# Substitution paced by the projections, a block of the joins by VectorE's transposes, and attention's position biases scaled block by block

## The chip, the cores and the metric

The kernel runs on one core of one Trainium2 chip. The core's engines each work through a queue of their own: TensorE (PE, with its weight loads shown as PEld), VectorE (DVE), ScalarE (ACT), GpSimd (POOL) and SyncE (SP), which here mostly issues DMA transfers. An instruction waits for semaphores that other engines or transfers raise; whatever is queued behind it on its engine waits too. The metric is the time of one execution on the device, in microseconds (us).

## The reference

Two layers run over 1024 tokens of width 1024 in fp32. Layer 0 mixes by a gated MLP (half the width) and by a gated DeltaNet (the other half), layer 1 by differential attention; each layer then has an MLP (square of relu, width 4096) and a gated addition of per-layer embeddings (PLE). What the change touches:

```python
# gated DeltaNet, per head and chunk of c = 64 tokens (4 heads, 16 chunks)
a = where(strict, einsum(k_beta, k) * decay, 0)   # strictly lower triangular
t_mat = a + eye(c)
u = solve_triangular(t_mat, v_beta)               # unit diagonal, lower
w = solve_triangular(t_mat, k_beta * exp(gc))
...                                               # then a scan over the chunks with a state
# differential attention, per head h of 8 (two softmaxes r = 0, 1), blocks of 128 queries
logits = q @ k.T - slopes[h] * dist               # slopes[h] = 2 ** -(h + 1)
logits = where(dist >= 0, logits, -inf)
attn = softmax(logits[0]) - lam * softmax(logits[1])
o = attn @ v
# MLP
h = h + square(relu(rms_norm(h) @ w_mlp1)) @ w_mlp2
```

## The kernel before

**Matmuls.** Nearly all time goes to products in three passes (`mm3`, L76 is the line of every matmul, L79 that of every transpose on TensorE): weights and activations are split into a high and a low part, and high x high, high x low and low x high are added up in PSUM. A weight's parts are made by `split` (L222 to L224): ScalarE casts the high part (L223), VectorE subtracts it to get the low part (L224). A tile of a weight (`w`, or `g` for the MLP's combined weights) is therefore ready only when an instruction on ScalarE and one on VectorE have run, in their places in those queues.

**Order.** A scheduler gives each engine its order from priorities and estimated times; the class `Ordered` (L48 to L90) adds constraints of issue order. `behind(inst, mark)` says that `inst` may be issued only after the instruction `mark` was issued on its own engine; it carries no semaphore for data. `pe.mark` is the name of the matmul written last. `floor` puts all matmuls of a group behind the group before.

**Layer 0's mixing** (`even_mix`, from L1231) has two kinds of work. The projections of the layer are a stream of *fill units* (small groups of `mm3`, `proj_qkv`, `proj_z`, `proj_uv`), which `pump(n)` (L1825) issues in order up to number n. The DeltaNet's own work is written between them, and with `run` (L1852) at high priority (EARLY = 3000). The counts of units issued in the stages are FILLA, FILLB, FILLC and FILLD (L35).
- `ahead(c)` (L1568 to L1607) makes the triangular system of each 128-token block c (two chunks); TensorE's `pd`, `pk`, `pkk`; the strictly lower blocks `am` lie in the tile `ring`. Its diagonal blocks of 32x32 are stored to `diag` (L1605) and the whole to `am_dram` (L1606), through SyncE's queue.
- `solve()` (L1612 to L1642) loads all 128 diagonal blocks, one per partition, into `work` (L1617, two transfers, for `x` and `a`), and issues loads of off-diagonal blocks, `ay` (L1621) and `a64` (L1628). It then inverts the blocks by forward substitution, all on VectorE: 30 columns, each a multiply `outer` (L1634) and an addition into `work` (L1635). Each depends on the one before. Two transposes of 128x1024 (L1640, L1641) give `dt` and `d`, the inverses block by block and their transposes.
- `merge()` (L1644 to L1712) joins 32x32 inverses to 64x64 and these to 128x128. At the first level, `py` = (off-diagonal block) x (inverse); then `pz` for p = 0 and 1, the two halves of the blocks: the product `pz[z0]` = d-transposed x `ay` is the joined block. For p = 0 a second product, `pz[z1]` = `ay`-transposed x d, gives the same block transposed. VectorE copies `pz[z0]` into `xt` (L1689, tile name `xts`), ScalarE copies `pz[z1]` into `xn` (L1691). The second level does the same with blocks of 64 (`py` and `yt` L1700, `pz` and the copies L1709), and stores the result to `xt_dram`. All products here are plain fp32 of 32x32 or 64x64; each shows as two matmul records. The names `quad[u][0]` (z0) and `quad[u][1]` (z1) are 32-partition strips of the half u.
- `prep(c)` and `step(c)` then run the scan over the blocks, with the rest of the projections as fill. VectorE also does the convolution behind some projections (`cx` L1353, `t` L1359, `qkv` L1362).

**The MLP** (`mlp`, from L290) multiplies by seven products of half-size blocks; `product2(2)` (L542) is its last one, and its sums go into `acc` (L284 and the additions behind it).

**Attention** (`attention`, from L873) keeps the position biases in one tile `al` (128x1024): GpSimd writes distances by `iota` (L880) and sets what lies in the future to -1e30 by `affine_select` (L881). As the slope halves from head to head, VectorE multiplies the whole of `al` by 0.5 at each head's first block (L1005, `b == 0 and r == 0`). For each block b of 128 queries and each r, `logits` runs the products `qk` and one VectorE operation that adds `al` and takes the minimum (`lg` and `nm`, L1016); block b reads the columns of `al` from (7-b)*128 on. ScalarE takes the exponential (L1019), VectorE combines the two (L1025 to L1027), TensorE transposes and multiplies by the values (`po`). `olo` (L1074) is the low part of a head's transposed result.

## Time and profile before

| | |
|---|---|
| three runs | 2529.52, 2530.80 and 2535.22 us, median 2530.80 |
| the profiled execution | 2532.05 us |
| its span in the trace | 2530.3 us, at a granted TensorE clock of 0.999 |
| 0 to 143 us | first projections and `ahead` |
| 143 to 188 us | substitution beside projections: TensorE busy 42.23 of 45 us, granted clock 0.96 |
| 188 to 250 us | joins and the first scan steps: TensorE busy 60.38 of 62 us, clock 0.97 |
| 250 to 440 us | rest of layer 0's mixing: 188.31 of 190 us, clock 1.00 |
| 440 to 1112 us | layer 0's MLP, from 936 us on its last part: 669.73 of 672 us |
| 1300 to 1700 us | seven of attention's heads: 395.97 of 400 us |

A profile row such as "L1005 DVE TENSOR_SCALAR al<-al x8" names the line, the engine, the operation, the tile written and the tiles read, and how many there were. In a list by time the first two numbers are the start and the duration, in us from the span's start, and "[2.77 <-DVE w L224]" says that the engine had been idle for 2.77 us and which instruction's end released it. In the chain of waits each row is a start, a length and what the chain spent it on; "SPq" is SyncE's queue, "issue" is time for which the profile shows no cause. Durations of neighbouring instructions overlap, since an engine starts the next one before the last has written back: what an instruction costs its engine is the distance from its start to the next start.

### The profile page before, as it was taken

How to read it: one execution, taken by the hardware profiler on the slowest of the kernel's cores; microseconds unless marked ns; L12 is line 12 of the kernel's file. 1: busy time of each engine (PE TensorE's matmuls, PEld its weight loads, DVE VectorE, ACT ScalarE, POOL GpSimd, SP SyncE). 2: the span in 40 equal slices, each digit the busy share in tenths (PEclk: the TensorE clock that was granted, in tenths of full speed). 3: DMA queues.
4: the chain of work that ended last, by engine and by line, in shares of the span. 5: the costliest groups of instructions: out<-in, count | busy, mean ns of one | idle time of the engine just before them, and what ended most of it. 6: DMA issues, size and time to landing. Idle time of an engine off the chain costs nothing.

```text
span 2530.3 us, 40003 instructions
## 1 busy us (share of the span) xinstructions
PE 2507.7 (99%) x14046; PEld 2149.1 (85%) x14046; DVE 1834.4 (72%) x3606; ACT 1307.2 (52%) x2635; POOL 259.9 (10%) x227
## 2 busy tenths in 40 slices
PE   9999999999999999999999999999999999999999
PEld 7998998888888878888999999988778888888887
DVE  7867665697676888656577777787887677787586
ACT  6634464565455434544466666555654555445452
POOL 0210220000000000000334333310000000000000
PEclk9999999999999999999999999999999999999999
DMA  7454436456557756553211111147466558655651
GB/s 238 131 155 109 142 105 197 130 193 227 163 179 263 236 169 206 179 162 113 79 48 52 50 47 43 59 139 260 139 218 203 175 183 282 216 184 185 202 178 59
DMA packets 310481, 398.48 MB, mean 157 GB/s; under 512 B 43428, under 2 KB 179592, under 8 KB 310280
## 3 DMA queue, kind: packets, MB, share of 16 engines
q1 hardware_dynamic: 309720, 395.40, 48.5%
q8 instruction: 110, 1.80, 0.3%
q14 instruction: 91, 0.75, 0.1%
q10 hardware_dynamic: 560, 0.53, 0.1%
HBM read 289.40 MB, written 106.43 MB: 156 GB/s over the span
## 4 chain that ended last, share of the span: by engine, by line
PE 92%; DVE 3%; DMA 2%; ACT 1%; issue 1%; SPq 0%; POOL 0%; ACTq 0%; DVEq 0%; POOLq 0%
PE mm L76 79%; PE po L76 3%; PE qk L76 2%; PE aux L76 2%; PE tr L79 2%; DMA raw<-in_w_ple_gate_dram 1%; DVE w L224 0%; DMA guv<-uv_dram 0%; PE aux L79 0%; DVE lg L1016 0%; PE pks L76 0%; PE pkq L76 0%; DMA work<-diag 0%; PE pd L76 0%; PE pkk L76 0%
## 5 line engine op out<-in xcount | busy, mean ns | idle before, releaser
L76 PE MATMUL mm<-g,w 128*128 128x512 f32 x2592 | 603.4, 394 | 1.6 <-DVE acc L284 1.2
L223 ACT CAST w<-raw 128x512 fp32r<-128x512 f32 x598 | 365.5, 618 | 463.5 <-PE mm L76 381.3
L76 PEld LDWEIGHTS mm<-g,w 128*128 128x128 f32 x2592 | 486.0, 188 | 116.7 <-ACT g L223 1.6
L76 PE MATMUL mm<-hi,w 128*128 128x512 f32 x1728 | 555.5, 397 | 0.3 <-ACT hi L1226 0.3
L76 PE MATMUL mm<-w,hi 128*128 128x256 f32 (+2 forms) x2528 | 506.7, 296 | 3.0 <-DVE w L224 3.0
L224 DVE TENSOR_TENSOR w<-raw,w 128x512 fp32r<-128x512 f32 x534 | 364.8, 690 | 181.5 <-ACT w L223 171.0
L76 PEld LDWEIGHTS mm<-w,hi 128*128 128x128 f32 x2528 | 401.4, 189 | 16.4 <-DVE w L224 3.4
L76 PEld LDWEIGHTS mm<-hi,w 128*128 128x128 f32 x1728 | 325.0, 189 | 74.3 <-ACT hi L1226 0.7
L76 PE MATMUL mm<-w,lo 128*128 128x256 f32 (+2 forms) x1264 | 370.1, 293 | 0.0
L76 PE MATMUL mm<-lo,w 128*128 128x512 f32 x864 | 341.3, 395 | 0.9 <-DVE lo L1227 0.9
L76 PE MATMUL mm<-t,w 128*128 128x512 f32 x1152 | 270.9, 394 | 1.2 <-ACT w L223 1.2
L76 PEld LDWEIGHTS mm<-t,w 128*128 128x128 f32 x1152 | 216.2, 188 | 52.8 <-ACT w L223 1.6
L76 PEld LDWEIGHTS mm<-w,lo 128*128 128x128 f32 x1264 | 238.6, 189 | 5.5
L76 PEld LDWEIGHTS mm<-lo,w 128*128 128x128 f32 x864 | 162.9, 189 | 37.0 <-DVE lo L1227 1.4
L224 DVE TENSOR_TENSOR g<-graw,g 128x512 fp32r<-128x512 f32 x216 | 147.3, 686 | 9.4 <-DMA gd<-g 8.4
L223 ACT CAST g<-graw 128x512 fp32r<-128x512 f32 x216 | 132.6, 617 | 28.8 <-PE mm L76 6.7
L1019 ACT ACTIVATE lg<-lg,nm 128x128 f32<-128x128 f32 (+7 forms) x128 | 99.4, 777 | 83.8 <-DVE nm L1016 77.4
L260 POOL TENSOR_TENSOR r<-ms,mhalf 128x4 f32<-128x4 f32 x12 | 13.3, 1108 | 1077.3 <-DVE ms L258 1050.1
L350 ACT ACTIVATE g<-g 128x512 f32<-128x512 f32 x96 | 60.5, 631 | 116.2 <-DVE g L284 109.3
L1016 DVE CUSTOM_DVE_ANT_0 lg<-qk,al 128x512 f32<-128x512 f32 (+3 forms) x128 | 75.1, 589 | 35.2 <-PE qk L76 31.7
L224 POOL TENSOR_TENSOR w<-raw,w 128x512 fp32r<-128x512 f32 x64 | 84.6, 1345 | 112.2 <-ACT w L223 56.9
L76 PE MATMUL mm<-ohi,w 128*128 128x512 f32 x256 | 85.2, 400 | 0.4 <-ACT ohi L1073 0.4
(348 smaller groups left out, 3587.3 us busy)
## 6 DMA issues: line engine op xcount, KB each, us to landing
raw<-in_w_mlp_dram SPq DMA_DIRECT2D x352, 256.0 KB, 3.0
graw<-gd SPq DMA_DIRECT2D x224, 256.0 KB, 2.8
gd<-g SPq DMA_DIRECT2D x192, 256.0 KB, 3.1
raw<-in_w_ple_gate_dram SPq DMA_DIRECT2D x76, 256.0 KB, 3.5
acc<-h_dram SPq DMA_DIRECT2D x64, 256.0 KB, 4.1
keep<-in_w_mlp_dram SPq DMA_DIRECT2D x64, 256.0 KB, 4.1
raw<-in_w_in_e_dram SPq DMA_DIRECT2D x60, 256.0 KB, 3.9
h_dram<-acc SPq DMA_DIRECT2D x48, 256.0 KB, 2.8
```

The lines of the kernel that those rows point to most:

```text
L76: self._next(self.engine.matmul(*a, **k))
L79: self._next(self.engine.transpose(*a, **k))
L223: self.nc.scalar.copy(hi, src)
L224: (lo_engine or self.nc.vector).tensor_tensor(lo, src, f32(hi), ALU.subtract)
L260: nc.gpsimd.tensor_tensor(r, ms, self.mhalf[:, 0:4], ALU.pow)
L350: nc.scalar.activation(g, src, AF.Relu)
L1016: nc.vector.tensor_tensor_reduce(out=lg[:, k0:k1], in0=ps[:, : k1 - k0], in1=al[:, u0 + k0 : u0 + k1], scale=-1.0, scalar=3.0e38 if c == 0 ...
L1019: nc.scalar.activation(lg[:, :n], lg[:, :n], AF.Exp, bias=nm[:, r, nch - 1 : nch], scale=-1.0, accum_out=me.sums[:, b, r : r + 1])
```

## The change

Three things are changed.

*Substitution.* FILLA goes from 36 to 62 and is shared over NC + 7 = 15 slots, so six slots of fill units alone follow the last `ahead`; FILLB goes from 64 to 36 and FILLC from 24 to 26. The solver's ten stages are written without high priority. In columns 1, 4, 7 and so on the multiply is held, in issue order, behind the matmul written last.

*Joins.* The 32 products `pz[z1]` for p = 0 and ScalarE's two copies out of them go; VectorE transposes `pz[z0]` (two halves of 32x512, each block of 32x32 for itself) into `xn`.

*Position biases.* `al` is scaled not as a whole at a head's first block, but by the 128 columns that a block reads first, at each block with r == 0: 64 operations of 128x128 in the place of 8 of 128x1024. `iota` is held, in issue order, behind the last matmul of the MLP written before it.

```diff
-FILLA, FILLB, FILLC, FILLD = 36, 64, 24, 31
+FILLA, FILLB, FILLC, FILLD = 62, 36, 26, 31
...
         ps = product2(2)
+        self.mlp_mark = self.pe.mark
...
-        nc.gpsimd.iota(al, pattern=[[1, S]], ...)
+        inst = nc.gpsimd.iota(al, pattern=[[1, S]], ...)
+        self.pe.behind(inst, self.mlp_mark)
         nc.gpsimd.affine_select(al, al, ...)
...
-                if b == 0 and r == 0:
-                    nc.vector.tensor_scalar(al, al, 0.5, None, ALU.mult)
+                if r == 0:
+                    new = al[:, (NB - 1 - b) * P : (NB - b) * P]
+                    nc.vector.tensor_scalar(new, new, 0.5, None, ALU.mult)
...
-                nc.vector.tensor_tensor(o, a[...], x[...], ALU.mult)
+                inst = nc.vector.tensor_tensor(o, a[...], x[...], ALU.mult)
                 nc.vector.tensor_tensor(x[:, j + 1 :, 0:j], x[:, j + 1 :, 0:j], o, ALU.add)
+                if j % 3 == 1:
+                    self.pe.behind(inst, self.pe.mark)
                 if j % 3 == 0:
                     yield
...
                 for n, u in itertools.product(range(16), range(2)):
-                    z0, z1 = quad[u]
+                    z0 = quad[u][0]
                     product(pz[z0, n], lhsT=d[z0, 16 * p + n], rhs=ay[p][z0, n])
-                    if p == 0:
-                        product(pz[z1, n], lhsT=ay[p][z0, n], rhs=d[z0, n])
                 last = self.pe.mark
                 for u in range(2):
                     nc.vector.tensor_copy(xt[quad[u][0], p, :, 32:64], pz[quad[u][0]])
                 for u in range(2 * (p == 0)):
-                    nc.scalar.copy(xn[quad[u][1], :, 0:32], pz[quad[u][1]])
+                    nc.vector.transpose(xn[quad[u][1], :, 0:32], pz[quad[u][0]])
...
-        for i, n in enumerate(share(FILLA, NC + 1)):
+        for i, n in enumerate(share(FILLA, NC + 7)):
             if i < NC:
                 run(systems[i], False)
-            if i:
+            if 0 < i <= NC:
                 run(systems[i - 1], False)
             self.pe.slot()
             pump(done + n)
         for n in share(FILLB, 10):
-            run(solver, False)
+            next(solver)
             self.pe.slot()
             pump(done + n)
-        run(solver, False)
+        next(solver, None)
```

More of the change, by code (lines that the diff above doesn't have):

```diff
@@ L879, in attention @@
         al = self.slot("B", [P, S], F32, "al")
-        nc.gpsimd.iota(al, pattern=[[1, S]], base=-(S - P), channel_multiplier=-1, allow_small_or_imprecise_dtypes=True)
+        inst = nc.gpsimd.iota(al, pattern=[[1, S]], base=-(S - P), channel_multiplier=-1, allow_small_or_imprecise_dtypes=True)
+        self.pe.behind(inst, self.mlp_mark)
         nc.gpsimd.affine_select(al, al, pattern=[[-1, S]], base=S - P, channel_multiplier=1, compare_op=ALU.is_ge, fill=-1.0e30)
@@ L1633, in solve @@
                 o = t[:, 0 : n * j].rearrange("p (i n) -> p i n", n=j)
-                nc.vector.tensor_tensor(o, a[:, j + 1 :, j : j + 1].to_broadcast([P, n, j]), x[:, j : j + 1, 0:j].to_broadcast([P, n, j]), ALU.mult)
+                inst = nc.vector.tensor_tensor(o, a[:, j + 1 :, j : j + 1].to_broadcast([P, n, j]), x[:, j : j + 1, 0:j].to_broadcast([P, n, j]), ALU.mult)
                 nc.vector.tensor_tensor(x[:, j + 1 :, 0:j], x[:, j + 1 :, 0:j], o, ALU.add)
+                if j % 3 == 1:
+                    self.pe.behind(inst, self.pe.mark)
                 if j % 3 == 0:
```

## The prediction

> **What bounds the kernel now.** I read the page first, then TensorE's table of waits, then the chain of waits by stretch, then the instruction lists of VectorE, SyncE and TensorE around each edited place, and last the written order of the changed kernel's instructions against that of the kernel before.

> ```profile
> PE 2507.7 (99%) x14046; PEld 2149.1 (85%) x14046; DVE 1834.4 (72%) x3606; ACT 1307.2 (52%) x2635; POOL 259.9 (10%) x227
> ```

> ```profile
> PE 92%; DVE 3%; DMA 2%; ACT 1%; issue 1%; SPq 0%; POOL 0%; ACTq 0%; DVEq 0%; POOLq 0%
> ```

> TensorE is busy for 99% of the span and carries 92% of the chain that ended last. Work taken from another engine is worth nothing in itself; only places where TensorE waits, or runs slowly, can pay. The table of waits names them (total, times, longest):

> ```profile
> PE mm L76 <- DVE w L224: 3.2, 3, 2.8
> PE tr L79 <- DVE olo L1074: 1.8, 3, 0.7
> PE pz L76 <- issue: 1.6, 1, 1.6
> PE qk L76 <- DVE nm L1016: 1.5, 2, 0.8
> ```

> ```profile
> PE mm L76 <- DVE g L224: 0.5, 1, 0.5
> ```

> Each of these five lies at an edit: `w` in the substitution, `pz` in the joins, `g` behind the position biases' first scaling, `nm` and `olo` in attention. All other waits are left as they were, so whatever the change is worth is found in these few microseconds.

> **The change part by part.** TensorE's instructions keep their order everywhere except around the substitution, in the joins (32 products fewer; each fp32 product of 32x32 shows as two matmul records, so 64 of 192 records go) and by small shuffles in two attention heads. The number of projection units issued by the end of the joins stays: 36+64+24+31 = 155 before, 62+36+26+31 = 155 after.

> (a) *Substitution.* The chain of waits from the last diagonal blocks on:

> ```profile
> 142.80 3.67 DMA am_dram<-ring
> 146.49 0.31 SPq L1621
> ...
> 150.40 6.70 DMA work<-diag
> ...
> 163.68 0.70 DVE w L224
> 164.42 23.03 PE mm L76 x179
> ```

> and TensorE's list at the wait:

> ```profile
> 161.14 0.52 PE L76 MATMUL mm<-w,hi 128*128 128x256 f32 x3
> 164.42 0.58 PE L76 MATMUL mm<-w,hi 128*128 128x256 f32 x1 [2.77 <-DVE w L224]
> ...
> 167.36 0.40 PE L76 MATMUL mm<-w,lo 128*128 128x256 f32 x1
> 167.57 0.42 PE L76 MATMUL mm<-w,hi 128*128 128x256 f32 x2
> ```

> The solver runs with high priority, so its dependent multiplies and adds stand in VectorE's queue ahead of a weight's low part (`w`, L224), whose ScalarE half was long done; it starts at 163.68, and TensorE, out of operands since its last start at 161.38, goes on at 164.42. Lost: 3.04 us less one ordinary matmul (0.12) = 2.92. The 14 matmuls from 164.42 to 167.57 then take 3.15 us, 225 ns each; the remaining 165 of the chain's 179 take 164.42+23.03-167.57 = 19.88 us, 120 ns each. That is 14 x 105 ns = 1.47 more: 4.4 in all. The change lets the solver run at ordinary priority, holds every third multiply behind the last matmul then issued, and puts 26 more projection units (six slots of them with nothing else in them) ahead of it, so that its input no longer has to be waited for. The new wait is one of issue order alone: behind a paced multiply VectorE's queue can stand only until TensorE has *issued* a matmul, and what queues there are low parts that TensorE needs several matmuls later. On SyncE, the `ay` load (L1621, 146.49) stood waiting for the store of `am_dram` from 142.80 on, ahead of the last `diag` stores is moved behind the loads of `work`, so the solver's data can land some 3 us sooner; a `uv_dram` store of a finished tile stands there in its place. Nothing else of the solver is on the path: its result is wanted by `py`, for which the 26 units make up. I take -4.4, with a remaining wait of 0 to 0.3 when a low part still falls behind two solver operations; the far ends are 0 (wait merely moved) and -4.4.

> (b) *The joins' block.* Chain of waits, and the ordinary rate of 128x512 matmuls from a long undisturbed stretch:

> ```profile
> 187.46 2.14 PE py L76 x128
> 189.60 5.31 PE mm L76 x22
> 194.91 1.77 PE pz L76 x119
> 196.68 1.61 issue
> 198.30 0.95 PE pz L76 x27
> 199.25 6.92 PE mm L76 x24
> 206.17 2.01 PE py L76 x64
> ```

> ```profile
> 498.57 290.65 PE mm L76 x1254
> ```

> The long stretch gives 290.65/1254 = 232 ns. Within the burst of 192 `pz` records TensorE stands still for 1.61 us and waits for nothing that the profile knows ("issue"), and the 24 matmuls behind it take 6.92 us where 24 x 0.232 = 5.57 is ordinary: 1.35 lost. The 22 behind the burst before it took 5.31 against 5.10. Each record is a weight load and a matmul, so 192 are 384 instructions in under 3 us of work, where the long stretch takes 232 ns for two; I read the stall as instructions that came too slowly. The removed 64 (a third of the burst) ran alongside the others, on other rows of the array, and cost next to nothing themselves (0.1). With 128 records left, the burst is as long as the `py` burst before it (128 records too, directly ahead of the 22 matmuls), which had no such row. I take -0.1-1.6-1.35 = -3.1; far ends +0 (stall recurs) and -3.2.

> (c) *What is late next: VectorE.* The copies and ScalarE's two copies into `xn` give way to two transposes of 32x512 on VectorE:

> ```profile
> 197.92 1.39 DVE L1689 COPY xts<-pz 32x512 f32<-32x512 f32 x2
> 199.34 0.75 DVE L1359 SCALAR_TENSOR_TENSOR t<-cx,cols,t 128x512 f32<-128x512 f32 x1
> 200.12 1.40 DVE L1689 COPY xts<-pz 32x512 f32<-32x512 f32 x2
> ```

> ```profile
> L1641 DVE STREAM_TRANSPOSE work<-work 128x1024 f32<-128x1024 f32 x1 | 2.2, 2160 | 0.0
> L1640 DVE STREAM_TRANSPOSE dt<-work 128x1024 f32<-128x1024 f32 x1 | 2.1, 2055 | 0.0
> ```

> These transposes take 2.06 to 2.16 us for 1024 columns; half as many columns by the same slope is about 1.05 each. In the changed order VectorE does, behind the first half's products, two copies (1.39), two transposes (2.1), a low part, a `qkv`, a `t` (0.69+0.69+0.75) and the second half's two copies (1.40): 7.0, less 0.4 of overlap at the joints = 6.6. TensorE meanwhile has the second half's products (about 1.0) and 21 matmuls of 0.232 = 4.9, together 5.9, and then its `py` needs the second half's copies. I take a new wait of 0.9 (0.7 and the hand-over). Its ends: 0 (transposes as cheap as the copies, 0.7) and 3.0 (2.1 each). Before, TensorE reached `py` at 206.17, 4.7 after those copies were done. Beyond it nothing is late: the joins' last result goes through a store and a load with a stretch of projections between.

> [...]

> (d) *The first scaling.*

> ```profile
> 942.77 0.69 DVE L1005 TENSOR_SCALAR al<-al 128x1024 f32<-128x1024 f32 x1
> 943.38 0.69 DVE L224 TENSOR_TENSOR g<-graw,g 128x512 fp32r<-128x512 f32 x1
> ```

> It stood directly ahead of a weight part for which TensorE waited (0.5 in the table); without it, `g` would start 0.61 sooner. In the changed kernel `iota` (GpSimd) is held behind the first MLP's last matmul, and the first head's eight scalings fall among that MLP's last sums, where VectorE has idle time before the next need. GpSimd's own queue is idle there (10% busy in all). -0.6; ends -0.6 and 0.

> (e) *Eight scalings for one in each head.*

> ```profile
> L1005 DVE TENSOR_SCALAR al<-al x8: 662/688/693, 942.8 to 1657.6; 128x1024 f32<-128x1024 f32 x8
> ```

> ```profile
> 1373.55 0.17 DVE L917 SCALAR_TENSOR_TENSOR ss<-ss,e 128x8 f32<-128x8 f32 x1
> 1373.63 0.17 DVE L1056 RECIPROCAL c<-sums 128x4 f32<-128x4 f32 x1
> ...
> 1374.63 0.69 DVE L1005 TENSOR_SCALAR al<-al 128x1024 f32<-128x1024 f32 x1
> 1375.47 0.29 DVE L1016 CUSTOM_DVE_ANT_0 lg<-qk,al 128x128 f32<-128x128 f32 x1
> ```

> The order of the changed kernel shows that the eight blocks are not spread over the head: they stand all eight together ahead of the head's first `lg`, where the single scaling stood. So nothing is relieved, and the pieces cost more than the whole: independent tiny operations start 0.08 apart (1373.55 to 1373.63), the whole one holds VectorE for 0.61 (942.77 to 943.38), so 128 columns lie near 0.08 + 0.53 x 120/1016 = 0.14; eight are 1.14, 0.53 more than the one. Ends: 0.08 each, no change; and 0.29 each, the duration of the 128x128 `lg` with no overlap, 2.32 or 1.7 more. At two heads TensorE waits for `nm` right behind the scaling and at one head for `olo` (the table's rows), and there it adds in full; at the other four TensorE has other matmuls to do. 3 x 0.53 = +1.6.

> [...]

> **Sum** on the profiled execution (2532.05, span 2530.3): -4.4 - 3.1 + 0.9 - 0.6 + 1.6 = -5.6, so 2526.4. The median of the runs shown is 2530.8, and the same difference gives **2525.2**, -0.22%.

> **The rivals.**
> 1. *A wait at `py` takes back the joins' gain.* Transposes of 32x512 cost as much as those of 128x1024 (2.1 each): the wait is 3.0 instead of 0.9, and the half rate follows (1.35): 2525.2 + 2.1 + 1.35 = 2528.6. For it: the four copies of only 32 partitions take 0.69, so partitions buy nothing and only the slope in columns is assumed.
> 2. *The stall only moves.* Instructions come too late again in the rearranged bursts, +1.6 + 1.35: 2528.1. Against it: the `py` burst of the same size ran through.
> 3. *The change doesn't do what it says.* The substitution is paced on paper, but a low part still queues behind the solver until TensorE runs dry: 2525.2 + 4.4 = 2529.6.
> 4. *Slower: eight scalings at full length in every head.* Each costs 0.29 with no overlap, 1.7 more per head, and TensorE feels it in all seven later heads, 12.0 instead of 1.6: 2535.6; a wait of that length is as long as the stall at 196.68, behind which 1.35 went at half rate, and if that follows at two heads it is 2538.3. It decides from (5.6+1.6)/7 = 1.03 us more per head on. Against it: the eight blocks don't overlap in data, and the tiny operations do overlap; four heads have other matmuls there.
> 5. *More than forecast.* No new wait in the joins and none felt in attention: 2525.2 - 0.9 - 1.6 = 2522.7.

> **How the numbers follow.** A measurement of this kernel can tell about 0.2%, 5.1 us, from no change, so the border of faster is 2525.7. The forecast has 0.50, its own range 2523.7 to 2526.7; rival 5 has 0.18, rivals 1 and 2 each 0.10, rival 3 0.06, rival 4 0.06. The range of 8 in 10 leaves out rival 4 and the tails: 2520.5 to 2530.5. Faster: rival 5 and four fifths of the forecast, 0.58. Slower: rival 4, 0.06, and the rest, 0.36, within 0.2%.

> **What would show it.** (a) No `mm <- DVE w` wait over 0.3 us near 160, 128x256 matmuls at 120 ns throughout. (b) No `issue` row in the `pz` burst, and the 128x512 behind it at 232 ns. (c) A `py <- DVE xts` wait of about 0.9; the two transposes near 1.05. (d) No `mm <- DVE g` near 943. (e) `al` rows x64, 0.13 to 0.15 apart, and `qk <- DVE nm` waits grown from 1.5 to about 2.6. I am wrong if the `work` load lands no sooner, if a wait longer than 0.9 appears in the joins, or if all heads show a wait for `nm`.

## The result and the profile after

The changed kernel took 2522.68 us (median of 6 runs, 2520.95 to 2524.40) against 2530.70 for the kernel before (6 runs, 2528.38 to 2535.22): a ratio of 0.9965, 95% interval 0.9952 to 0.9978. The medians lie 8.0 us apart; the ratio, which is worked out from all the runs, says 0.35% faster. The forecast was 2525.2, the range 2520.5 to 2530.5. The profiled execution took 2522.26 with a span of 2520.5, 9.8 less than the span before.

The page of the changed kernel, busy time and the chain that ended last:

```profile
PE 2503.7 (99%) x13982; PEld 2145.8 (85%) x13982; DVE 1839.6 (73%) x3664; ACT 1307.8 (52%) x2633; POOL 258.2 (10%) x227
...
PE 95%; DVE 2%; ACT 1%; DMA 1%; issue 0%; POOL 0%; ACTq 0%; DVEq 0%; POOLq 0%
```

TensorE has 64 records less and 3 points more of the chain; the solver's chain through DMA and VectorE is out of it. TensorE's table of waits (line numbers are up to 5 higher than before):

```profile
PE tr L79 <- DVE olo L1078: 2.3, 3, 1.2
PE qk L76 <- ACT lg L1023: 1.8, 2, 0.9
...
PE mm L76 <- ACT g L223: 1.0, 1, 1.0
...
PE mm L76 <- DVE w L224: 0.2, 1, 0.2
...
```

Of the five rows of before, `w` fell from 3.2 to 0.2, `pz <- issue` (1.6) and `g` (0.5) are gone, `olo` grew from 1.8 to 2.3, and the wait at `qk` grew from 1.5 to 1.8 and is now put down to ScalarE. The wait of 1.0 for ScalarE's half of `g` (at 922.55) is new, and one of 1.2 for `acc` (L284, at 931.33 before) is gone. The chain of waits through the substitution and the joins:

```profile
140.44 48.91 PE mm L76 x385
189.35 2.14 PE py L76 x128
191.49 4.81 PE mm L76 x20
196.30 2.14 PE pz L76 x128
198.44 5.06 PE mm L76 x21
203.50 2.44 PE py L76 x64
205.95 2.75 PE mm L76 x11
```

No wait of TensorE is listed between 130 and 250 us; 20 matmuls of 128x512 in 4.81 us are 240 ns each, 21 in 5.06 are 241 ns. No half rate is left: the granted clock is 1.00 there.

How the difference grows along the span is read from stretches that both chains show, in which the instructions are the same: the 1254 matmuls of the first MLP, the 73 behind it and the 103 of the output projection behind attention.

```profile
489.95 290.65 PE mm L76 x1254
```

```profile
1216.79 8.61 PE mm L76 x73
```

```profile
1742.90 23.91 PE mm L76 x103
```

They start at 489.95 (before: 498.57), 1216.79 (1226.31) and 1742.90 (1752.07): 8.6 us are won in layer 0's mixing, 0.9 more around the first MLP's end, 0.35 is lost in attention, and the rest of the 9.8 comes behind it, where nothing was changed.

### The profile page after: what moved, and what is told of

Read it like the earlier page. It is cut to its first block, busy times and chain, and to the rows that moved or that the text cites. A ratio compares the mean times of both kernels' runs of the same rounds, so it can differ in the third digit from the quotient of the medians.

```text
span 2520.5 us, 39929 instructions
## 1 busy us (share of the span) xinstructions
PE 2503.7 (99%) x13982; PEld 2145.8 (85%) x13982; DVE 1839.6 (73%) x3664; ACT 1307.8 (52%) x2633; POOL 258.2 (10%) x227
## 4 chain that ended last, share of the span: by engine, by line
PE 95%; DVE 2%; ACT 1%; DMA 1%; issue 0%; POOL 0%; ACTq 0%; DVEq 0%; POOLq 0%
PE mm L76 83%; PE po L76 3%; PE aux L76 2%; PE qk L76 2%; PE tr L79 2%; DVE lg L1020 0%; DMA guv<-uv_dram 0%; PE aux L79 0%; PE pkk L76 0%; PE pks L76 0%; PE pkq L76 0%; PE pd L76 0%; ACT t L1466 0%; DVE lg L1031 0%; ACT lg L1023 0%
## 5 line engine op out<-in xcount | busy, mean ns | idle before, releaser
L76 PE MATMUL mm<-g,w 128*128 128x512 f32 x2592 | 603.4, 394 | 1.1 <-ACT g L223 1.0
L76 PEld LDWEIGHTS mm<-g,w 128*128 128x128 f32 x2592 | 486.0, 188 | 116.1 <-ACT g L223 1.4
L76 PE MATMUL mm<-hi,w 128*128 128x512 f32 x1728 | 554.0, 396 | 0.3 <-ACT hi L1230 0.3
L76 PE MATMUL mm<-w,hi 128*128 128x256 f32 (+2 forms) x2528 | 504.3, 295 | 0.0
L224 DVE TENSOR_TENSOR w<-raw,w 128x512 fp32r<-128x512 f32 x534 | 365.1, 690 | 179.9 <-ACT w L223 172.6
L76 PEld LDWEIGHTS mm<-w,hi 128*128 128x128 f32 x2528 | 400.6, 188 | 13.5
L76 PEld LDWEIGHTS mm<-hi,w 128*128 128x128 f32 x1728 | 324.2, 188 | 73.8 <-ACT hi L1230 0.7
L76 PE MATMUL mm<-w,lo 128*128 128x256 f32 (+2 forms) x1264 | 369.9, 293 | 0.0
L76 PE MATMUL mm<-lo,w 128*128 128x512 f32 x864 | 340.8, 395 | 0.9 <-DVE lo L1231 0.9
L76 PE MATMUL mm<-t,w 128*128 128x512 f32 x1152 | 270.9, 394 | 1.2 <-ACT w L223 1.2
L76 PEld LDWEIGHTS mm<-t,w 128*128 128x128 f32 x1152 | 216.2, 188 | 52.8 <-ACT w L223 1.6
L76 PEld LDWEIGHTS mm<-w,lo 128*128 128x128 f32 x1264 | 238.0, 188 | 5.3
L76 PEld LDWEIGHTS mm<-lo,w 128*128 128x128 f32 x864 | 162.4, 188 | 37.0 <-DVE lo L1231 1.4
L224 DVE TENSOR_TENSOR g<-graw,g 128x512 fp32r<-128x512 f32 x216 | 147.0, 684 | 8.7 <-DMA gd<-g 8.1
L224 POOL TENSOR_TENSOR w<-raw,w 128x512 fp32r<-128x512 f32 x64 | 84.2, 1339 | 111.0 <-ACT w L223 64.8
L76 PE MATMUL mm<-ohi,w 128*128 128x512 f32 x256 | 85.4, 400 | 0.6 <-ACT ohi L1077 0.4
```

Of the source, the lines that this page charges most:

```text
L76: self._next(self.engine.matmul(*a, **k))
L224: (lo_engine or self.nc.vector).tensor_tensor(lo, src, f32(hi), ALU.subtract)
```

## The experiments

All were timed beside the kernel before; "the wait for w" and "the issue row" are those of the tables and chains of their own profiled executions. Theories at the outset: mine was the sum of the prediction with the joins' stall put down to the supply of instructions; rivals were that extra units, not pacing, do the work in the substitution; that the stall hangs on the place in the stream, or on the second products themselves, and not on the burst's length; and that attention doesn't pay.

**The substitution alone.** FILLA to FILLC, slots, ordinary priority and pacing as changed; joins and biases as before.

```diff
-FILLA, FILLB, FILLC, FILLD = 36, 64, 24, 31
+FILLA, FILLB, FILLC, FILLD = 62, 36, 26, 31
...
-            run(solver, False)
+            next(solver)
...
+                if j % 3 == 1:
+                    self.pe.behind(inst, self.pe.mark)
```

> The kernel before with the substitution's part of the change alone (more projection units ahead, ordinary priority, every third multiply held in issue order). My theory: this part carries the largest share, 4.4 us (2530.7 to about 2526.3, ratio 0.9983): no wait of TensorE for w near 160, and the joins behind it keep their 1.6 us issue row and slow matmuls. Rival: the parts only work together, because the rearranged stream moves the stall of the joins as well; then this kernel gains 7 us or more (0.997), and no issue row is left.

Measured: 2524.92, ratio 0.9981 (0.9973 to 0.9990). There was no wait for `w` in the substitution, and the chain shows the full burst of 192 records without a stall:

```profile
196.42 2.21 PE pz L76 x145
198.63 5.05 PE mm L76 x21
```

(In such bursts some records are missing from the trace, so the count runs short of 192.) In its rows the rival is right: the part takes the joins' stall away too, though the joins were untouched. The 7 us or more that it went with did not come (5.4, interval 2.5 to 6.8). A burst of 192 is therefore not too long in itself.

**The joins alone.** The second products out, two transposes in.

```diff
-                    if p == 0:
-                        product(pz[z1, n], lhsT=ay[p][z0, n], rhs=d[z0, n])
...
-                    nc.scalar.copy(xn[quad[u][1], :, 0:32], pz[quad[u][1]])
+                    nc.vector.transpose(xn[quad[u][1], :, 0:32], pz[quad[u][0]])
```

> The kernel before with the joins' part alone (no second products, two transposes on VectorE). My theory, a burst of 192 records outruns the supply of instructions: the issue row of 1.6 us goes, the 128x512 matmuls behind run at 232 ns, the gain is about 3 us (ratio 0.9988), and the 2.8 us wait for w near 160 stays. The transposes take 0.72 each and py waits less than 0.5 us. Rival: the stall comes at a place in the stream and not from the burst's length; then the issue row stays at about 1.6 us and the time is within 0.5 us of before.

Measured: 2525.67, 0.9980 (0.9971 to 0.9989). No issue row; 30 matmuls behind the burst took 7.17 us. The wait for `w` stayed, but it was 1.3 and not 2.8. Alone, the two parts gain 5.4 and 4.6 where the changed kernel gains 8.0 with all three, and neither chain has an issue row: both remove the same stall.

**The biases alone.**

```diff
+        self.pe.behind(inst, self.mlp_mark)
...
-                if b == 0 and r == 0:
-                    nc.vector.tensor_scalar(al, al, 0.5, None, ALU.mult)
+                if r == 0:
+                    new = al[:, (NB - 1 - b) * P : (NB - b) * P]
+                    nc.vector.tensor_scalar(new, new, 0.5, None, ALU.mult)
```

> The kernel before with the biases' part alone (64 scalings of 128 columns, iota behind the first MLP's last matmul). The step on record (each head pays 0.53 us more, three heads feel it): +1.6 in attention and -0.6 at 943 us, +1.0 in all (1.0004). Rival that the changed kernel's trace suggests: the eight hold VectorE for 1.09 us in the place of 0.84, because the lg behind needs only the first of them, and the wait that grows by 0.12 at qk shrinks by 0.12 at po: attention within 0.3 us of before, and -0.8 at 943 us, so 0.5 to 0.8 us faster (0.9997).

Measured: 2528.95, 0.9996 (0.9987 to 1.0004): no difference that can be told. The +1.0 of the step on record lies at the upper end of this interval, so the time alone doesn't exclude it. Its waits in attention are those of the changed kernel (`olo` 2.3, `lg` 1.8); the wait for `g` is gone, and the wait for `acc` ahead of it is 1.6 here and 1.2 before.

**The burst cut in two**, second products kept.

```diff
+                if p == 0:
+                    yield
+                    yield
+                    last = self.pe.mark
             yield
...
-        chunk(none, merger, FILLC, "pppp")
+        chunk(none, merger, FILLC, "pppppp")
```

> The kernel before with the joins' second products and ScalarE's copies kept, but with the pz burst cut in two: 12 projection matmuls (2.8 us) stand between the 128 records of the first half and the 64 of the second. Theory of the instructions' supply: each of the two bursts is short enough, no issue row is left, the 128x512 matmuls behind run at 232 ns, gain about 3 us less what the later joins lose. Rival (the second products themselves, or ScalarE's copies, hold TensorE up): the 1.6 us issue row stays within one of the two bursts.

Measured: 2526.70, 0.9985 (0.9976 to 0.9994). The chain of waits:

```profile
195.32 1.22 PE pz L76 x82
196.53 2.99 PE mm L76 x12
199.52 1.13 PE pz L76 x64
200.65 5.95 PE mm L76 x25
```

No stall, 238 ns per matmul behind it, with the second products and ScalarE's copies still in the kernel. The stall is not theirs. (The profiled execution was the slowest of the ten, 2531.95; it had a wait of 1.9 for `w` ahead of the joins.)

**The extra units alone**: counts and slots as changed, high priority kept, no pacing.

> The kernel before with the moved projection units alone (62, 36, 26, 31 and 15 slots); the solver keeps its high priority and isn't paced. If the extra units are what helps (the solver's data is there before it is asked for), TensorE's wait for w near 160 is gone, as in the paced kernel. If priority and pacing are what helps, the solver's operations still stand ahead of weights' low parts and a wait of 1 to 3 us remains. On the joins: the burst's 384 instructions, counted in TensorE's program, run from 2869 to 3253; if instructions come in blocks of 256 with borders at 2958 and 3214 (as the place of the stall in the kernel before says), two borders lie in the burst, more than 46 instructions behind its start, and the stall of 1.6 us is still there. Time: 2530 in this case, 2527 if the wait goes.

Measured: 2528.86, 0.9993 (0.9984 to 1.0001). TensorE's only wait between 143 and 215 us:

```profile
PE pz L76 <- issue: 1.7, 1, 1.7
```

The wait for `w` is gone without any pacing, and the stall is there, as the count of instructions said it would be: the burst starts 14 instructions earlier than before, not later. The 22 matmuls behind it took 7.71 us in place of 5.10. With the stall still there, the time can't be told from that of before.

**The changed kernel without pacing**, that is with the two lines of `j % 3 == 1` left out.

> The changed kernel without the pacing (no multiply held behind a matmul); everything else as changed. If the ordinary priority with the extra units is enough: no wait for w over 0.3 us near 160 to 190 and 2522.7 as the changed kernel. If the pacing carries the gain: solver operations come in a run as soon as their data is there, a wait for w of 1 to 3 us with slow matmuls behind it, 2524 to 2527.

Measured: 2523.40, 0.9970 (0.9959 to 0.9982), the time of the changed kernel. No wait between 143 and 215.

**Ordinary priority and pacing alone**, counts of units as before.

> The kernel before with ordinary priority and pacing of the solver alone; the projections' counts stay at 36, 64, 24 and 31. If pacing by itself removes the substitution's wait: no wait for w over 0.3 us near 160. If the extra units are needed: the solver's operations follow their data as before and a wait for w of 1 to 3 us is left. The burst of the joins stands at the same place in the stream as before (2883 to 3267), so the issue row of 1.6 us and the slow matmuls behind it stay in both cases: 2528 to 2530, at most 0.1% faster than before.

Measured: 2531.82, 1.0004 (0.9995 to 1.0013). Its waits in the same stretch:

```profile
PE pz L76 <- issue: 1.9, 1, 1.9
PE mm L76 <- DVE w L224: 1.4, 1, 1.4
```

Pacing by itself gains nothing. With the old counts the solver's first operation started at 156.10 here, at 157.12 in the kernel before, and in both the first low part of a weight followed some 20 solver operations later.

**The stream moved by 52 instructions.** 13 idle products of 32x32 stand at the very start of the kernel before; they compute nothing that is used.

```diff
+        for _ in range(13):
+            T.pe.matmul(idle[0:32, 0:32], lhsT=T.ident[0:32, 0:32], rhs=T.ident[0:32, 0:32], start=True, stop=True)
         first = Weight(...)
```

> The kernel before with 13 idle products of 32x32 (52 instructions) at its very start, where TensorE has nothing to do; everything else is as before, only that later instructions stand 50 places further on in the stream (the pz burst from 2933 to 3317 in place of 2883 to 3267). Theory of blocks of 256 with borders at 2958 and 3214 and a sequencer that reads some 46 ahead while matmuls are long: the first border is now passed in front of the burst, 2.4 us earlier, so the block behind the second is there in time: no issue row, the matmuls behind the burst at 232 ns, about 3 us faster. Rival (a burst of 192 records always outruns its instructions, or it is no matter of instructions): the issue row stays at 1.6 us, no change.

Measured: 2527.53, 0.9992 (0.9983 to 1.0001).

```profile
190.96 1.39 PE pz L76 x93
192.35 0.86 issue
193.21 1.01 PE pz L76 x51
194.22 6.82 PE mm L76 x22
```

The stall is halved, not gone: 0.86 in place of 1.61, with the half rate still behind it (6.82 in place of 5.10). The place in the stream matters, but the border isn't passed as early as I had worked it out; that some 46 instructions are read ahead was an estimate of mine, and no run shows it.

**The stream moved back.** The kernel with the substitution alone, which had no stall, and 50 such idle products (200 instructions).

> The kernel with the substitution's part alone, which showed no stall with the same burst of 192 records, with 50 idle products of 32x32 (200 instructions) at its start: the burst runs from 3136 to 3520 with borders at 3214 and 3470, 78 and 334 instructions behind its start, nearly as in the kernel before (75 and 331). Theory of blocks: the issue row of about 1.6 us and slow matmuls behind it come back, about 3 us slower than the same kernel without the shift (2524.9 to 2528). Rival: the stall went with the substitution's wait and has nothing to do with the place in the stream; then no issue row and 2525.

Measured: 2535.56, 1.0024 (1.0015 to 1.0033).

```profile
204.96 1.80 PE pz L76 x120
206.76 1.98 issue
208.74 0.72 PE pz L76 x25
209.46 6.46 PE mm L76 x21
```

The stall is back, and 21 matmuls take 6.46 where the same kernel without the shift took 5.05. The time is 10.6 above that kernel and not 3, because the idle products delay everything behind them: the burst starts 8.5 us later (204.96 and 196.42). From there to the end of the `py` behind it (217.98 and 206.11) another 3.3 are lost, which is what the theory asked for.

**Scalings truly spread.** In the changed kernel, blocks 1 to 7 are held behind the matmul written last, so that one scaling stands ahead of a head's first `lg`; the changed kernel itself ran beside it.

```diff
-                    nc.vector.tensor_scalar(new, new, 0.5, None, ALU.mult)
+                    inst = nc.vector.tensor_scalar(new, new, 0.5, None, ALU.mult)
+                    if b:
+                        self.pe.behind(inst, self.pe.mark)
```

> The changed kernel again, as the measure for the two kernels beside it on the same chip: 2522 to 2524 (0.9967).

> The changed kernel with the scalings of blocks 1 to 7 held in issue order behind the matmul written last, so that one and not eight stands ahead of a head's first lg. If the eight in a row are what TensorE waits for at two heads' starts (1.16 and 0.36 us each) and at olo (1.6), VectorE reaches lg 0.95 sooner there and these waits shrink by about 0.9 at each: 2 to 3 us faster than the changed kernel, 2520 to 2521. If ScalarE's exponential and the aT copy behind it set those waits anyway, it is the same within 0.5 us.

Measured: 2523.93 for the changed kernel (0.9965, 0.9952 to 0.9977), 2524.18 with the spread (0.9966, 0.9953 to 0.9978): the same. TensorE's list at the same head of the kernel before, of the changed one and of the spread one, in this order:

```profile
1434.33 0.36 PE L76 MATMUL qk<-ks,qh 128*128 128x256 f32 x1 [0.76 <-DVE nm L1016]
1434.52 0.28 PE L76 MATMUL qk<-ks,ql 128*128 128x256 f32 x1
1435.01 1.16 PE L76 MATMUL po<-v,aT 128*128 128x128 f32 x8 [0.21 <-ACT aT L1037]
```

```profile
1424.60 0.36 PE L76 MATMUL qk<-ks,qh 128*128 128x256 f32 x1 [0.89 <-ACT lg L1023]
1424.79 0.28 PE L76 MATMUL qk<-ks,ql 128*128 128x256 f32 x1
1425.15 1.05 PE L76 MATMUL po<-v,aT 128*128 128x128 f32 x7
```

```profile
1423.77 0.36 PE L76 MATMUL qk<-ks,qh 128*128 128x256 f32 x1 [0.30 <-DVE nm L1022]
1423.96 0.28 PE L76 MATMUL qk<-ks,ql 128*128 128x256 f32 x1
1424.91 1.16 PE L76 MATMUL po<-v,aT 128*128 128x128 f32 x8 [0.67 <-ACT aT L1043]
```

The wait at `qk` goes 0.76, 0.89, 0.30, and the wait at `po` two instructions later 0.21, none listed, 0.67: what one gives the other takes. Over all of attention the rows `olo`, `qk` and `po` add up to 3.7 us before, 4.1 in the changed kernel and 3.3 in the spread one: the 0.9 that were expected came at `olo` alone (2.3 to 1.4), too little to be told in the time.

**Spread, and the joins' transposes behind the second half's copies.**

```diff
                 for u in range(2):
-                    nc.vector.tensor_copy(xt[quad[u][0], p, :, 32:64], pz[quad[u][0]])
-                for u in range(2 * (p == 0)):
-                    nc.vector.transpose(xn[quad[u][1], :, 0:32], pz[quad[u][0]])
+                    inst = nc.vector.tensor_copy(xt[quad[u][0], p, :, 32:64], pz[quad[u][0]])
+                pz0 = pz0 if p else pz
+                for u in range(2 * (p == 1)):
+                    self.pe.behind(nc.vector.transpose(xn[quad[u][1], :, 0:32], pz0[quad[u][0]]), inst.ins.name)
```

> The same with the two 32x512 transposes of the joins held behind the second half's copies as well. The gap of 0.2 us within py at 203.66 and the 0.1 ahead of it go, nothing else moves, since the transposes' result is wanted only 7 us later: 0.3 us faster in the trace, not to be told in the time.

Measured: 2523.71, 0.9963 (0.9949 to 0.9976). `py` took 2.06 in place of 2.44 us, as expected; the time can't tell it.

## Why the prediction was right, and where not

The direction held and the time lay in the range, though outside the forecast's own 2523.7 to 2526.7. It lies on rival 5's number (2522.7), but by luck: rival 5 asked for no new wait in the joins and none felt in attention, and both cost something (0.4 and 0.35). By its steps:

**(a) The substitution, -4.4.** The mechanism is in the main as told: the wait went because the solver's data came earlier and a weight's low part no longer stood so far behind the solver's operations. In the changed kernel SyncE's queue and VectorE's list show it:

```profile
147.64 0.95 SPq L1621 DMA_DIRECT2D work<-diag  x2
148.64 2.13 SPq L1625 DMA_DIRECT2D ay<-am_dram  x4
```

```profile
153.77 0.20 DVE L1638 TENSOR_TENSOR outer<-work 128x30 f32<-128x30 f32 x1 [1.34 <-DMA work<-diag]
...
157.93 0.69 DVE L224 TENSOR_TENSOR w<-raw,w 128x512 fp32r<-128x512 f32 x1 [0.28 <-ACT w L223]
```

`ay` now stands behind `work`; the solver starts at 153.77 instead of 157.12 and the first low part runs at 157.93 instead of 163.68. As executions differ in where TensorE is at a given time, the start is better counted from TensorE's last group of `pkk`. With the old counts of units 20 solver operations stand ahead of the first low part, and the wait follows that distance one for one (all in us):

| old counts of units | last `pkk` | solver starts | distance | wait for `w` |
|---|---|---|---|---|
| kernel before | 140.51 | 157.12 | 16.6 | 2.8 |
| burst cut | 141.62 | 157.41 | 15.8 | 1.9 |
| pacing alone | 140.89 | 156.10 | 15.2 | 1.4 |
| joins alone | 141.78 | 156.90 | 15.1 | 1.3 |
| biases alone | 138.88 | 153.51 | 14.6 | 0.8 |
| stream moved | 141.09 | 154.87 | 13.8 | none |

With the new counts there is no wait at 13.1 (units alone, 22 operations ahead), 13.6 (unpaced, 21 ahead) and 14.4 (changed kernel, 13 ahead).

But two things in my step were off. The pacing, which I had counted in, was not needed in these executions: without it the wait is gone too (2523.40), and by itself it gains nothing (2531.82). With the new counts it does bring the low parts forward (13 operations ahead in place of 21); whether that helps when the data lands late was not tested. And 4.4 is the loss of one execution. The wait for `w` was 2.8 in the profile of before, and in the other profiled executions with the old counts of units 1.3 (joins alone), 0.8 (biases alone), 1.9 (burst cut), 1.4 (pacing alone) and none (stream moved): 1.4 on average of the six. The half rate that made 1.47 of the 4.4 is the granted clock, the third number from the end in these two stretches of the kernel before, behind the wait and behind the joins' stall:

```profile
164.30:167.50 3.20, 3.08 (x14) 3.08 (x15) 3.17 (x8) 0.00 (x0) 0.00 (x0) 0.50 0.52 130
198.40:201.60 3.20, 3.20 (x33) 2.65 (x33) 3.04 (x6) 1.15 (x2) 0.00 (x0) 0.50 0.55 86
```

The trace's clock records have 0.50 from 164.19 to 167.60 and from 198.32 to 201.74, 3.41 us each. At this place it came only behind the two longest waits for `w` (2.8 and 1.9); behind that of 1.3 us TensorE went on at full rate at once. Against the median this step was therefore worth about 2 and not 4.4: a rough estimate, 1.4 and a half rate of about 1.5 in two of the six. No profile with the new counts shows this wait (substitution alone, units alone, the changed kernel, unpaced, spread), which may be why the changed kernel's runs lie within 3.5 us of each other and those of before within 6.8.

**(b) The joins, -3.1.** The stall and the half rate behind it went, as forecast. The 64 records cost next to nothing, as I took it: a `pz` burst of 192 without a stall took 2.21 us (the substitution alone), one of 128 took 2.14 (the changed kernel). Before, the two products ran alongside each other (starts 194.84 and 194.85, 0.21 each); on which rows of the array, no trace shows. The reason that I gave was half right. It is the instructions' supply, but not the burst's length alone: the same burst of 192 ran through in the kernel with the substitution alone and when it was cut, its stall was halved when the stream was moved by 52 instructions, and it stalled again when the stream was moved by 200. The shorter burst ran through in the joins alone, whose place in the stream was the old one. So in the changed kernel the stall is removed twice, by the shorter burst and by the new place, and neither part's own gain can be added to the other's. The size hung on the execution, too: stall and half rate together cost 2.1 to 4.5 us in the four profiles in which the burst stalled near its old place (before, units alone, biases alone, pacing alone).

```profile
q8 instruction: 110, 1.80, 0.3%
```

```profile
q8 instruction: 111, 1.82, 0.3%
```

These are transfers of 16384 bytes each, 110 of them for the 28092 matmuls and weight loads of before and 111 for 28292: one for every 256, at 64 bytes each. (That this queue is TensorE's is read from these counts.) In all six stalls TensorE goes on 2.3 to 2.6 us after such a transfer has started, in the kernel before at 195.87 and 198.30. That transfer starts 0.96 us into the burst. With the stream moved by 52 instructions it starts 0.08 ahead of the burst, 1.04 sooner and not the 2.4 that I had worked out, and the stall is 0.75 shorter. With the substitution alone and in the changed kernel it starts 2.2 ahead of the burst, and there is no stall. In the joins alone it starts 1.1 us into the burst, but the shorter burst is over 1.1 us later.

**(c) The new wait at `py`, +0.9.** Mis-sized: the transposes took 0.72 each and not 1.05, as much as the copies, the lower of the two ends that I gave.

```profile
198.96 1.44 DVE L1696 STREAM_TRANSPOSE work<-pz 32x512 f32<-32x512 f32 x2
```

The second half's copies ran until 203.82; `py` started at 203.50 and took 2.44 instead of 2.01, so the wait is about 0.4 and lies inside the burst. Held behind the copies, the transposes cost nothing (2.06). They aren't the whole reason for the wait, though: the substitution alone has no transposes and its `py` took 2.42, the joins alone have them and theirs took 2.06. The other work in VectorE's queue there decides too. No half rate followed (granted clock 1.00 from 203.50 to 206.00); rival 1 had neither of its conditions. Elsewhere the clock did fall to 0.50: behind the waits of 2.8 and 1.9 us at `w`, and behind five of the six stalls, of 0.9 to 2.0 us.

**(d) The first scaling, -0.6.** Right on average: the row for `g` is gone. One execution can't tell the size, because waits for `acc` and for ScalarE's half of `g` come and go beside it. Between 890 and 965 us TensorE's listed waits add up to 1.6 us on average in the eight profiles with the whole scaling (0.4 to 2.2) and to 0.9 in the six with the scaling by blocks (0.2 to 1.6).

**(e) Eight scalings for one, +1.6.** This is the step that failed. VectorE's list at the head of the changed kernel:

```profile
1423.07 1.17 DVE L1009 TENSOR_SCALAR al<-al 128x128 f32<-128x128 f32 x8
1424.16 0.28 DVE L1020 CUSTOM_DVE_ANT_0 lg<-qk,al 128x128 f32<-128x128 f32 x1
```

The eight hold VectorE for 1.09, 0.136 each, as worked out (0.14). But the single scaling held it for 0.84 there (1374.63 to 1375.47), not for the 0.61 that I took from 943 us: the `lg` behind it had to wait until all of `al` was written, whereas behind the eight it needs only the first. So VectorE lost 0.25 per head and not 0.53. And "there it adds in full" was wrong: the lists above show that TensorE has two waits in a row at that place, the second of them on ScalarE's `aT`, which takes up what the first gives or costs. 0.13 more at `qk` was 0.21 less at `po`. Only `olo` grew, by 0.5 in the table. The biases' part alone measured 0.9996 (0.9987 to 1.0004).

The sum by these sizes, about -2 for (a), -3 for (b), +0.4, -0.7 and +0.35, is about -5; measured were 8.0 between the medians, with an interval of 5.6 to 12.1 by the ratio. What lies between the two isn't settled by these runs, but part of it goes with the granted clock. Of the runs of the kernel before beside the experiments, 11 had a clock of 1.000 and a median of 2527.9, 42 had 0.999 and 2530.0, 30 had 0.998 and 2531.7, and 3 had 0.997 and 2534.3. Of the changed kernel's 11 runs, 7 had 1.000 and a median of 2522.3, and 4 had 0.999 and 2524.8. At equal clock the two kernels lie 5.6 and 5.3 apart; the rest of the 8.0 goes with the lower clock that the kernel before has in most of its runs. How much of that the sum already holds is open.

Rivals 2 and 4 did not come about. Rival 3 was nearest to the truth in one point: pacing without the extra units gains nothing.

## What to carry to other kernels

A wait in one profiled execution is a sample; where it hangs on when a DMA transfer lands, look at more than one execution before its size goes into a sum. Where an engine stands still and waits for nothing, look at when its instructions were transferred. Parts that remove the same stall can't be added, and a part may remove one just by moving later instructions to another place in the stream: test a part alone and the others without it. Before a delay is added to the end, look one wait further down the engine's list: if the next wait is on another chain, it can swallow the delay, and the mending too.

## What the runs showed that was not expected

- TensorE can stand still for 0.9 to 2.0 us within a burst of small products with nothing that the chain of waits names. It went on 2.3 to 2.6 us after a transfer of 16384 bytes of instructions had started. Whether it stands still depends on how many instructions stand ahead of the burst since the start of the program: 52 more at the start changed 1.61 to 0.86 us, 200 more brought 1.98 into a kernel that had none.
- Behind such a stall the granted clock mostly fell to 0.50, for 3.41 us (before) or 6.83 us (units alone, biases alone): 22 matmuls of 128x512 took 7.71 us in place of 5.10 after 1.7 us of standing still. In another execution it did not, and 24 took 5.77 in place of 5.57 after 1.9 us. The same holds for plain waits: none of it behind 1.3 and 1.4 us at `w`, but 3.41 us at 0.50 (392.08 to 395.49, in the kernel with the stream moved) behind 1.45 us at `pgm`. So the length of the gap alone doesn't decide it.
- A transpose of 32x512 on VectorE, out of PSUM, took 0.72 us, 1.4 ns per column; those of 128x1024 in SBUF took 2.07 and 2.14 us, 2.0 to 2.1 ns per column.
